# Attention's scores, values and gate filler as three streams through all heads, and a second buffer of squares in the projections of a hybrid block

## The chip, the core and the metric

The kernel runs on one core of one Trainium2 chip. The core has five engines, each with its own queue of instructions: TensorE (PE, matrix products and transposes, writing to PSUM), VectorE (DVE), ScalarE (ACT), GpSimd (POOL) and SyncE (SP, which issues the DMAs between memory and SBUF). The metric is the device time of one execution in microseconds (us); less is better. Times of runs are given as a median of several, and a profile is of one further execution.

## The reference

One layer of a streaming encoder over 1024 positions of width 1024, in float32:

```
hn = rms_norm(x);  u = hn @ w_in          # split for MLA, FoX, SSM and three gates
y_a = mla_branch(u_mla) @ w_br_mla        # 8 heads of 96, values of 64
y_b = fox_branch(u_fox) @ w_br_fox        # 8 heads of 64, decay added to the scores
y_c = ssm_branch(u_ssm) @ w_br_ssm        # conv, Mamba-2 scan, gated norm
g = sigmoid(u_gate + b_gate)
x = x + (g0 * y_a + g1 * y_b + g2 * y_c) @ w_out
x = x + conv_ffn(rms_norm(x))
```

Both attentions are a softmax over earlier positions (causal by chunks of 64 in MLA, strictly causal in FoX), `p = softmax(q k' + mask)`, `out = p v`. FoX normalises each head's q and k by the root of its mean square; z, the gate of the SSM branch, is a plain projection.

## The kernel before

All products keep float32's precision by splitting an operand into a high and a low part and adding three products. Lists of PE's instructions are in the order in which the program issues them (the stages run under a manual schedule for PE); the order on ACT, DVE, POOL and SP is made by the framework's scheduler from the program and its dependencies.

**Projections of FoX q, k and of z (lines 1016 to 1132).** Four column chunks of 512 (z first half, q, k, z second half) times eight token tiles: 32 units of 24 matmuls (`fx_part`, L798). Behind each unit of q or k, `qk_sum` squares the tile on ACT (L1053) into a buffer `fsq`, of which there is one, and sums it by heads on DVE (L1054). Behind each pair of tiles `qk_pair` makes 1/root of 16 columns on DVE (`rsqrt`, L157 to L168: two integer operations, a scaling and three Newton steps of three operations) and scales the tiles (L1063); `qk_out` transposes them on PE (L1070) into one of two `tp` banks, which ACT (L1074) and DVE (L1075) empty. `out_z` puts a tanh into the same buffer `fsq` (L1046). Beside the units run the split of the next chunk's weights (`load_part`; L139 on ACT, L140 on DVE), sums of weights for the last stage on POOL (`down_sums`, L939 to L942) and, in the third and fourth chunk, sums of the normalised input for the convolution (`token_sums`, L957 to L977, on POOL, ACT and DVE).

`small` (L246) is a tile of 128 x 8 x 24 numbers with the raw forget gates and time steps. It is last read at L836, before the units.

**Attention (L1403 to L1611).** 16 heads, the eight of MLA first. A head has four units `jp`, each of two rows of query tiles (128 queries). `score_row` computes the row's scores in one or two chunks (L1453) into one of two score banks `s`, with three products in MLA and two in FoX, where the mask is one more small product (L1463), held back until the next score row or values step. Then, through a list `later` of things to issue at nominal times: the row's maximum on DVE (L1464), the exponential with its sum on ACT (L1466) into one of six buffers `pm`, and 1/sum on DVE with the scaling on POOL (L1470, L1471). `values` transposes the two rows of a unit on PE (L1529) into two `tp` banks, groups of up to two key pairs at a time; ACT and DVE split them (L1534, L1535); products with the head's values `vv` follow two key pairs later (`PVLAG`; L1494 to L1502) into one bank `o` whose halves alternate; ACT and DVE empty it (L1507, L1512), and a DMA stores it to `att_d`.

The **filler** `all_fill` is the gate projection: 24 column blocks of two halves, each half eight steps of three matmuls (L1337), in pieces of two steps here. It has one bank, so that behind a half it yields up to four times without work until ACT has taken the bank (L1317). What attention doesn't use runs beside the SSD scan, and the rest alone behind it.

A generator yields the nominal cost of what it has just issued, in us. `merge` runs the streams of one unit to their end: always the one whose share of its own cost is least. A unit merges the scores of unit n, the values of unit n - 2, and fill for 0.50 of the two costs:

```
cost_s(jp, n=3) = sum(n * max(b - a, 256) / 2400 over the chunks of both rows) + 0.1
cost_v(jp)      = 0.88 * jp + 0.33 + 0.39
```

Over the four units of a head the columns sum to 4736, so that scores are 5.92 with three products and 3.95 with two; a FoX row yields 0.05 more than its products (`yield c + 0.05`, L1480). Values yield 0.11 for each transpose and 0.44 for each key pair's products. A fill step of three matmuls counts 0.65.

A head's q and k are loaded one head ahead, when the scores of unit 0 begin, and its `vv` when those of unit 3 begin (two buffers).

Of the kernel before, what the change touches and what calls it, by code (L numbers as in the profile page):

```python
# [11 lines left out]
F32 = mybir.dt.float32  # L12
# [9 lines left out]
P = 128  # L22
# [20 lines left out]
def block_kernel(ctx: ExitStack, tc: tile.TileContext, x, positions, norm_mix_g, w_in, b_gate,  # L43
# [951 lines left out]
    def conv_first():  # L995
# [17 lines left out]
        c_first["raw"], c_first["S"] = r, S_  # L1013
        yield

    with ExitStack() as px:
        xp = px.enter_context(TP("xp", 2))

        def load_part(w, n, j, c0):

# [21 lines left out]
            return lambda k: w[0][i][:, k, :] if k < 4 else w[k // 2 - 1][i][:, k % 2, :]  # L1042

        def out_z(p, t, zc):
            th = xp.tile([P, 512], F32, name=uid("th"), tag="fsq", bufs=1)
            A.activation(th, p, AF.Tanh, scale=0.5)  # L1046
            zt = xp.tile([P, 512], F32, name=uid("zt"), tag="fqn", bufs=4)
            V.scalar_tensor_tensor(out=zt, in0=th, scalar=1.0, in1=p, op0=ALU.add, op1=ALU.mult)
            SY.dma_start(z_d[t * P:(t + 1) * P, zc:zc + 512], zt)

        def qk_sum(p, ss):
            sq = xp.tile([P, 512], F32, name=uid("fsq"), tag="fsq", bufs=1)
            A.activation(sq, p, AF.Square)  # L1053
            V.reduce_sum(ss, sq.rearrange("p (h d) -> p h d", d=64), axis=AX)  # L1054

        def qk_pair(ps, ss):
            v = xp.tile([P, 16], F32, name=uid("fv8"), tag="fv8")
            V.tensor_scalar(v, ss, 1.0 / 64, EPS, op0=ALU.mult, op1=ALU.add)
            r = xp.tile([P, 16], F32, name=uid("fr8"), tag="fr8")
            rsqrt(xp, r, v, 16)  # L1060
            for i, p in enumerate(ps):
                qn = xp.tile([P, 8, 64], F32, name=uid("fqn"), tag="fqn", bufs=4)
                V.tensor_mul(qn, p.rearrange("p (h d) -> p h d", d=64),  # L1063
                             r[:, 8 * i:8 * i + 8].unsqueeze(2).to_broadcast([P, 8, 64]))
                yield qn
# [20 lines left out]
        for n, (which, c0) in enumerate(chunks):  # L1086
# [12 lines left out]
            for t in range(NT):  # L1099
# [13 lines left out]
                if which > 2:  # L1113
                    out_z(p, t, 512 * (which - 3))
                    if behind:
                        qk_out(*behind.pop(0))
                elif t % 2 == 0:
                    ss = xp.tile([P, 16], F32, name=uid("fss"), tag="fss")
                    qk_sum(p, ss[:, 0:8])
                    p_even = p  # L1120
                else:
                    qk_sum(p, ss[:, 8:16])
                    behind += [(qn, which, t - 1 + i) for i, qn in enumerate(qk_pair((p_even, p), ss))]
# [277 lines left out]
                s_[2] += c  # L1401


    class Head:
        pass

# [80 lines left out]
    def values(o, jp, pn, me):  # L1487
# [32 lines left out]
        for k0 in range(0, jp + 1, 2):  # L1520
# [3 lines left out]
            for kp in range(k0, min(k0 + 2, jp + 1)):  # L1524
                pt, pl = a_tp.get()
                off = 0
                for k in (2 * kp, 2 * kp + 1):
# [7 lines left out]
                pl[0] = later(cs + 0.6, lambda th=th, tl=tl, pt=pt, off=off: V.tensor_sub(  # L1535
                    tl[:, :off], pt[:, :off], f32(th[:, :off])))
                pend.append((pv, kp, th, tl, pl, jp, done if kp == jp else None))
            yield cs
            while len(pend) > PVLAG:
                if pend[0][1] == 0 and clk[0] - t_done[0] < 1.0:  # L1540
                    yield 0.0
                run_pv()
                if len(pend) <= PVLAG and k0 + 2 <= jp:
                    tp_next.append(me[0])
                yield 0.44

# [17 lines left out]
    def cost_v(jp):  # L1564
        return 0.88 * jp + 0.33 + 0.39

    FILL_ATT = 0.50
    FILL_SSD = [11.3] * 8 + [12.0, 24.5]
    with ExitStack() as pt__:
        atp = pt__.enter_context(TP("atp", 2))  # L1570
        psp = pt__.enter_context(TP("psa", 1, space=PSUM))
        a_pm = Ring(atp, [P, S], F32, "pm", 6)
        a_nmx, a_rs = (Ring(atp, [P, 4], F32, n, 4) for n in ("nmx", "rs"))
        a_th, a_tl = (Ring(atp, [P, 512], F32R, n, PVLAG + 2) for n in ("pth", "ptl"))
        a_o1 = Ring(atp, [64, 256], F32, "o1", 1)
# [4 lines left out]
        with tc.manual_schedule(engines={mybir.EngineType.PE}):  # L1580
            names = [(br, h) for br in range(2) for h in range(8)]
            merge([], 5.0)
            units = [(n, jp) for n in range(16) for jp in range(4)]
            heads = {0: load_head(atp, *names[0])}
            load_values(atp, heads[0])
            done = []
            for n in range(len(units) + 2):
                st, share = [], 0.0
                if n < len(units):
                    hn_, jp = units[n]  # L1590
                    if jp == 0 and hn_ + 1 < 16:
                        heads[hn_ + 1] = load_head(atp, *names[hn_ + 1])
                    if jp == 3 and hn_ + 1 < 16:
                        load_values(atp, heads[hn_ + 1])
                    pn = []
                    done.append((heads[hn_], jp, pn))
                    share += cost_s(jp)
                    st.append((scores(heads[hn_], jp, pn), cost_s(jp, len(heads[hn_].passes))))
                if n >= 2:
                    share += cost_v(done[n - 2][1])  # L1600
                    me = []
                    me.append(values(*done[n - 2], me))
                    tp_next[:] = me
                    st.append((me[0], cost_v(done[n - 2][1])))
                merge(st, FILL_ATT * share)
            flush()
            while pend:
                run_pv()
                clk[0] += 0.44
                run_until(clk[0])  # L1610
            run_until(clk[0] + 3.0)  # L1611
# [748 lines left out]
```

## Time and profile before

| | |
|---|---|
| runs, median (lowest to highest of 3) | 2035.72 us (2033.51 to 2036.61) |
| the profiled execution, its own time | 2032.95 us |
| its span, first to last instruction | 2031.2 us |
| granted TensorE clock, mean | 0.996 |
| busy: PE, DVE, ACT, POOL | 1974.9, 1403.3, 960.4, 720.4 us |
| projections of q, k and z, roughly | 197 to 401 us |
| attention | 516 to 918 us |

The page of the profile gives busy times by engine, the span in slices, the chain that ended last, and groups of instructions by line. In a group's row stand the line, engine, operation, the tile written and the tile read, the count, then busy us and the mean in ns of one, then the idle time of the engine before them and who ended it. A row of the waits reads: engine and line that waited, what released it, us in total, times, longest. A row of the timeline has start and duration in us and, in brackets, the engine's idle time before it. A row of the windows has the stretch, its length, then the busy time of each engine with its number of instructions, the granted clock, the share of the DMA engines and GB/s.

### The profile page before, as it was taken

The numbers are of one execution on the slowest core, as the hardware profiler recorded it, in microseconds if no ns is written. First come the engines' busy times: TensorE is split into PE (matmuls) and PEld (weight loads), VectorE is DVE, ScalarE is ACT, GpSimd is POOL, SyncE is SP. The second block draws the span as 40 slices with busy tenths as digits, with TensorE's granted clock in tenths as the row PEclk, the third lists the DMA queues.
The fourth block names the chain that finished last, engine by engine and source line by source line (L and its number), as shares of the span: only waits on it lengthen the run. The fifth ranks groups of instructions, "written<-read, shape, count | busy, mean of one in ns | idle before, by whom it ended". The sixth has DMA issues, their size and how long they took to land.

```text
span 2031.2 us, 28367 instructions
## 1 busy us (share of the span) xinstructions
PE 1974.9 (97%) x10113; PEld 1669.2 (82%) x10113; DVE 1403.3 (69%) x2141; ACT 960.4 (47%) x1674; POOL 720.4 (35%) x670
## 2 busy tenths in 40 slices
PE   9999997999899999999999999999999999999999
PEld 8999886788788887887888878888888888888887
DVE  7777579589566566665885466558997787675655
ACT  5554322345555556656775232224544445454432
POOL 5033335164222222222332163000565444522655
PEclk9999999999999999999999999999999999999999
DMA  5167873333644445526553687432422211249675
GB/s 176 61 195 219 266 249 95 108 102 104 180 128 128 127 127 140 143 79 215 179 178 125 215 294 257 145 125 84 135 83 84 93 58 46 84 134 330 205 258 193
DMA packets 278263, 312.15 MB, mean 154 GB/s; under 512 B 19197, under 2 KB 209289, under 8 KB 278122
## 3 DMA queue, kind: packets, MB, share of 16 engines
q1 hardware_dynamic: 278120, 310.35, 48.8%
q8 instruction: 79, 1.29, 0.3%
q14 instruction: 62, 0.51, 0.1%
q10 hardware_dynamic: 2, 0.00, 0.0%
HBM read 217.17 MB, written 93.13 MB: 153 GB/s over the span
## 4 chain that ended last, share of the span: by engine, by line
PE 81%; DVE 8%; ACT 3%; issue 3%; DMA 3%; POOL 1%; SPq 0%; ACTq 0%; DVEq 0%; POOLq 0%
PE mm L1337 12%; PE dn L2307 10%; PE ybr L1875 7%; PE fx L798 7%; PE ua L1966 5%; PE cb L1187 5%; PE uc L1966 5%; PE ud L1966 4%; PE wo L2011 4%; PE s L1453 3%; PE tp L1529 3%; PE ub L1966 2%; PE fxv L188 2%; PE py L1720 1%; ACT pm L1466 1%
## 5 line engine op out<-in xcount | busy, mean ns | idle before, releaser
L1471 POOL TENSOR_SCALAR pm<-pm,rs 128x128 f32<-128x128 f32 (+7 forms) x128 | 96.8, 757 | 298.7 <-DVE rs L1470 224.0
L2307 PE MATMUL dn<-dr,dr 128*128 128x512 f32 x592 | 182.3, 389 | 0.0
L1337 PE MATMUL mm<-hnh,wh 128*128 128x512 f32 x384 | 160.2, 417 | 0.9 <-DVE o L1512 0.9
L1337 PE MATMUL mm<-hnh,wl 128*128 128x512 f32 x384 | 151.2, 394 | 0.0
L1337 PE MATMUL mm<-hnl,wh 128*128 128x512 f32 x384 | 150.8, 393 | 0.0
L1535 DVE TENSOR_TENSOR ptl<-tp,pth 128x512 fp32r<-128x512 f32 (+1 forms) x160 | 98.6, 633 | 52.6 <-ACT pth L1534 50.9
L2307 PEld LDWEIGHTS dn<-dr,dr 128*128 128x128 f32 x592 | 111.1, 188 | 23.2
L1464 DVE TENSOR_REDUCE nmx<-s 128x1 f32<-128x128 f32 (+7 forms) x128 | 95.5, 752 | 32.9 <-PE s L1453 18.6
L2307 PE MATMUL dn<-dr 128*128 128x512 f32 x296 | 115.2, 389 | 0.0
L1466 ACT ACTIVATE pm<-s,nmx 128x128 f32<-128x128 f32 (+7 forms) x128 | 94.7, 742 | 43.2 <-DVE nmx L1464 34.4
L1534 ACT ACTIVATE pth<-tp 128x512 fp32r<-128x512 f32 (+1 forms) x160 | 85.1, 554 | 48.0 <-PE tp L1529 47.8
L135 DVE TENSOR_TENSOR dr<-dr,dr 128x1024 fp32r<-128x1024 f32 x52 | 72.1, 1395 | 51.8 <-ACT dr L134 41.0
L135 DVE TENSOR_TENSOR wl<-S,wh 128x1024 fp32r<-128x1024 f32 x53 | 80.7, 1523 | 32.7 <-ACT wh L134 32.7
L1875 PE MATMUL ybr<-ah,wl 128*128 128x512 f32 x256 | 99.7, 389 | 1.1 <-DVE wl L135 1.1
L1875 PE MATMUL ybr<-ah,wh 128*128 128x512 f32 x256 | 99.7, 389 | 0.4 <-ACT wh L134 0.4
L1875 PE MATMUL ybr<-al,wh 128*128 128x512 f32 x256 | 99.6, 389 | 0.0
L134 ACT ACTIVATE wh<-wr 128x1024 fp32r<-128x1024 f32 (+1 forms) x45 | 40.3, 896 | 103.3 <-PE ybr L1875 51.9
L134 ACT ACTIVATE dr<-dr 128x1024 fp32r<-128x1024 f32 x52 | 54.8, 1061 | 71.6 <-PE dn L2307 51.6
L134 ACT ACTIVATE wh<-S 128x1024 fp32r<-128x1024 f32 x53 | 56.1, 1059 | 63.8 <-PE uc L1966 45.7
L1337 PEld LDWEIGHTS mm<-hnh,wl 128*128 128x128 f32 x384 | 72.4, 189 | 16.6
L1529 PE MATMUL tp<-ident,pm 128*128 128x128 f32 x576 | 81.3, 273 | 2.0 <-DVE ptl L1535 1.6
L1337 PEld LDWEIGHTS mm<-hnh,wh 128*128 128x128 f32 x384 | 72.7, 189 | 12.4 <-DVE o L1512 1.1
(594 smaller groups left out, 6170.7 us busy)
## 6 DMA issues: line engine op xcount, KB each, us to landing
dr<-act_d SPq DMA_DIRECT2D x99, 256.0 KB
wr<-in_w_in_dram SPq DMA_DIRECT2D x36, 512.0 KB
g_d<-t SPq DMA_DIRECT2D x24, 512.0 KB
gl<-g_d SPq DMA_DIRECT2D x24, 512.0 KB
wr<-in_ffn_w_up_dram SPq DMA_DIRECT2D x23, 512.0 KB
ws<-in_ffn_w_down_dram SPq DMA_DIRECT2D x22, 512.0 KB
wsum_d<-ws SPq DMA_DIRECT2D x22, 512.0 KB
act_d<-fa SPq DMA_DIRECT2D x22, 512.0 KB
```

Of the source, the lines that this page charges most:

```text
L134: i = A.activation(h, src, AF.Copy) if he is A else he.tensor_copy(h, src)
L135: return i, le.tensor_sub(l, src, f32(h))
L798: T.matmul(p, a(k), b(k), start=k == 0 and i == 0, stop=k == NK - 1 and i == 2)
L1187: T.matmul(ps, a, b, start=first and i == 0, stop=i == 11, skip_group_check=not first)
L1337: T.matmul(ps, a[:, k, :], b[half][:, k, :], start=(k == 0 and i == 0), stop=(k == NK - 1 and i == 2))
L1466: pl[0] = later(t1, lambda: A.activation(p_[:, 0:n * P], row, AF.Exp, bias=nmx[:, 0:1], accum_out=rs[:, 0:1]))
L1471: G.tensor_scalar(p_[:, 0:n * P], p_[:, 0:n * P], rs[:, 1:2], 0.0, op0=ALU.mult, op1=ALU.add)
L1529: T.transpose(pt[:, off:off + P], pn[qi][0][:, k * P:k * P + P], ident)
L1535: pl[0] = later(cs + 0.6, lambda th=th, tl=tl, pt=pt, off=off: V.tensor_sub(tl[:, :off], pt[:, :off], f32(th[:, :off])))
L1875: T.matmul(pss[half], w_[:, k, :], a_[k][:, hs], start=k == 0 and i == 0, stop=k == nk - 1 and i == 2)
L1966: T.matmul(ps, a, b, start=first and n == 0, stop=n == 11, skip_group_check=not first)
L2307: T.matmul(ps[m], a[:, ts_], b[:, 512:], start=first_ and j == 0 and q == 0, stop=j == NFH - 1 and q == 2, skip_group_check=not first_)
```

## The change

Three edits. **In the projections** the buffer `fsq` gets a second copy. Room for it comes from the columns of the roots: `fv8`, `fr8`, `rs_i`, `rs_v`, `rs_t` and `fss`, 16 columns each in two copies, are now slices of the tile `small`, handed out in turn by a class `Columns`. **In attention** the units' merges give way to one call of `weave`: `all_scores` runs through the rows of all heads, `all_values` through the units' values, and the filler beside them. `weave` always advances the stream with the least account, where an account grows by what was yielded over the stream's cost of a head (`scores_`, `values_`, `FILL_HEAD` with 5.4 in MLA and 7.2 in FoX), and begins at 0 for scores, at 0.62 for values and at -0.6 for fill. A stream that yields 0 lets the least of the others go once. Values can't start a unit before both of its score rows are placed. While a FoX mask is held, values go first if they are due within 0.04 heads. It ends when only fill is left. **The buffers** `pm` grow from six to eight. In `values`, the stream is marked as next also where no products are due behind a group's transposes.

```diff
--- before.py
+++ after.py
@@ -1013,8 +1013,22 @@
         c_first["raw"], c_first["S"] = r, S_
         yield
 
+    class Columns:
+
+
+        def __init__(self, t):
+            self.flat, self.tags, self.turn = t.rearrange("p t c -> p (t c)"), {}, {}
+
+        def tile(self, shape, dt, name, tag):
+            i = self.tags.setdefault(tag, len(self.tags))
+            self.turn[tag] = j = 1 - self.turn.get(tag, 1)
+            c0 = 16 * (2 * i + j)
+            t = self.flat[:, c0:c0 + 16]
+            return t if dt is F32 else t.bitcast(dt)
+
     with ExitStack() as px:
         xp = px.enter_context(TP("xp", 2))
+        xs_ = Columns(small)
 
         def load_part(w, n, j, c0):
 
@@ -1042,22 +1056,22 @@
             return lambda k: w[0][i][:, k, :] if k < 4 else w[k // 2 - 1][i][:, k % 2, :]
 
         def out_z(p, t, zc):
-            th = xp.tile([P, 512], F32, name=uid("th"), tag="fsq", bufs=1)
+            th = xp.tile([P, 512], F32, name=uid("th"), tag="fsq")
             A.activation(th, p, AF.Tanh, scale=0.5)
             zt = xp.tile([P, 512], F32, name=uid("zt"), tag="fqn", bufs=4)
             V.scalar_tensor_tensor(out=zt, in0=th, scalar=1.0, in1=p, op0=ALU.add, op1=ALU.mult)
             SY.dma_start(z_d[t * P:(t + 1) * P, zc:zc + 512], zt)
 
         def qk_sum(p, ss):
-            sq = xp.tile([P, 512], F32, name=uid("fsq"), tag="fsq", bufs=1)
+            sq = xp.tile([P, 512], F32, name=uid("fsq"), tag="fsq")
             A.activation(sq, p, AF.Square)
             V.reduce_sum(ss, sq.rearrange("p (h d) -> p h d", d=64), axis=AX)
 
         def qk_pair(ps, ss):
-            v = xp.tile([P, 16], F32, name=uid("fv8"), tag="fv8")
+            v = xs_.tile([P, 16], F32, name=uid("fv8"), tag="fv8")
             V.tensor_scalar(v, ss, 1.0 / 64, EPS, op0=ALU.mult, op1=ALU.add)
-            r = xp.tile([P, 16], F32, name=uid("fr8"), tag="fr8")
-            rsqrt(xp, r, v, 16)
+            r = xs_.tile([P, 16], F32, name=uid("fr8"), tag="fr8")
+            rsqrt(xs_, r, v, 16)
             for i, p in enumerate(ps):
                 qn = xp.tile([P, 8, 64], F32, name=uid("fqn"), tag="fqn", bufs=4)
                 V.tensor_mul(qn, p.rearrange("p (h d) -> p h d", d=64),
@@ -1115,7 +1129,7 @@
                     if behind:
                         qk_out(*behind.pop(0))
                 elif t % 2 == 0:
-                    ss = xp.tile([P, 16], F32, name=uid("fss"), tag="fss")
+                    ss = xs_.tile([P, 16], F32, name=uid("fss"), tag="fss")
                     qk_sum(p, ss[:, 0:8])
                     p_even = p
                 else:
@@ -1401,6 +1415,29 @@
                 s_[2] += c
 
 
+    def weave(streams):
+
+        st = [[g, lead, per] for g, lead, per in streams]
+        while any(e[0] is not fill for e in st):
+            s_ = min(st, key=lambda e: e[1])
+            if held:
+                v = [e for e in st if e[0] in tp_next]
+                if v and v[0][1] <= s_[1] + 0.04:
+                    s_ = v[0]
+                else:
+                    flush()
+            c = advance(s_[0])
+            if c == 0.0:
+                rest = [e for e in st if e is not s_]
+                if rest:
+                    s_ = min(rest, key=lambda e: e[1])
+                    c = advance(s_[0])
+            if c is None:
+                st.remove(s_)
+            else:
+                s_[1] += c / s_[2]()
+
+
     class Head:
         pass
 
@@ -1535,12 +1572,14 @@
                 pl[0] = later(cs + 0.6, lambda th=th, tl=tl, pt=pt, off=off: V.tensor_sub(
                     tl[:, :off], pt[:, :off], f32(th[:, :off])))
                 pend.append((pv, kp, th, tl, pl, jp, done if kp == jp else None))
+            if len(pend) <= PVLAG:
+                tp_next.append(me[0])
             yield cs
             while len(pend) > PVLAG:
                 if pend[0][1] == 0 and clk[0] - t_done[0] < 1.0:
                     yield 0.0
                 run_pv()
-                if len(pend) <= PVLAG and k0 + 2 <= jp:
+                if len(pend) <= PVLAG:
                     tp_next.append(me[0])
                 yield 0.44
 
@@ -1564,12 +1603,13 @@
     def cost_v(jp):
         return 0.88 * jp + 0.33 + 0.39
 
-    FILL_ATT = 0.50
+    FILL_HEAD = (5.4, 7.2)
+    LAG = 0.62
     FILL_SSD = [11.3] * 8 + [12.0, 24.5]
     with ExitStack() as pt__:
         atp = pt__.enter_context(TP("atp", 2))
         psp = pt__.enter_context(TP("psa", 1, space=PSUM))
-        a_pm = Ring(atp, [P, S], F32, "pm", 6)
+        a_pm = Ring(atp, [P, S], F32, "pm", 8)
         a_nmx, a_rs = (Ring(atp, [P, 4], F32, n, 4) for n in ("nmx", "rs"))
         a_th, a_tl = (Ring(atp, [P, 512], F32R, n, PVLAG + 2) for n in ("pth", "ptl"))
         a_o1 = Ring(atp, [64, 256], F32, "o1", 1)
@@ -1580,29 +1620,37 @@
         with tc.manual_schedule(engines={mybir.EngineType.PE}):
             names = [(br, h) for br in range(2) for h in range(8)]
             merge([], 5.0)
-            units = [(n, jp) for n in range(16) for jp in range(4)]
             heads = {0: load_head(atp, *names[0])}
             load_values(atp, heads[0])
-            done = []
-            for n in range(len(units) + 2):
-                st, share = [], 0.0
-                if n < len(units):
-                    hn_, jp = units[n]
-                    if jp == 0 and hn_ + 1 < 16:
-                        heads[hn_ + 1] = load_head(atp, *names[hn_ + 1])
-                    if jp == 3 and hn_ + 1 < 16:
-                        load_values(atp, heads[hn_ + 1])
-                    pn = []
-                    done.append((heads[hn_], jp, pn))
-                    share += cost_s(jp)
-                    st.append((scores(heads[hn_], jp, pn), cost_s(jp, len(heads[hn_].passes))))
-                if n >= 2:
-                    share += cost_v(done[n - 2][1])
-                    me = []
-                    me.append(values(*done[n - 2], me))
-                    tp_next[:] = me
-                    st.append((me[0], cost_v(done[n - 2][1])))
-                merge(st, FILL_ATT * share)
+            todo = []
+            at = [0, 0]
+
+            def all_scores():
+                for n in range(16):
+                    at[0] = n // 8
+                    for jp in range(4):
+                        if jp == 0 and n + 1 < 16:
+                            heads[n + 1] = load_head(atp, *names[n + 1])
+                        if jp == 3 and n + 1 < 16:
+                            load_values(atp, heads[n + 1])
+                        pn = []
+                        todo.append((heads[n], jp, pn))
+                        yield from scores(heads[n], jp, pn)
+
+            me = []
+
+            def all_values():
+                for n in range(64):
+                    at[1] = n // 32
+                    while n >= len(todo) or len(todo[n][2]) < 2:
+                        yield 0.0
+                    yield from values(*todo[n], me)
+
+            me.append(all_values())
+            tp_next[:] = me
+            scores_ = lambda: sum(cost_s(jp, 3 - at[0]) - 0.1 for jp in range(4))
+            values_ = lambda: sum(cost_v(jp) for jp in range(4))
+            weave([(all_scores(), 0.0, scores_), (me[0], LAG, values_), (fill, -0.6, lambda: FILL_HEAD[at[1]])])
             flush()
             while pend:
                 run_pv()
```

## The prediction

> **What bounds the kernel now.** I read the page first: TensorE is the engine that is nearly always busy, so time can only come from stretches in which it stands still, or from the order of its own work.
>
> ```profile
> span 2031.2 us, 28367 instructions
> PE 1974.9 (97%) x10113; PEld 1669.2 (82%) x10113; DVE 1403.3 (69%) x2141; ACT 960.4 (47%) x1674; POOL 720.4 (35%) x670
> ```
>
> Then the busy time by stretch: 305 to 362 us is the middle of the FoX and z projections (two rows), 520 to 918 us is attention, with the MLA heads in the first of its two rows and the FoX heads in the second, to within a head. Columns: length, then busy time of PE, PEld, DVE, ACT, POOL, then the granted clock.
>
> ```profile
> 305.00:335.00 30.00, 24.64 (x111) 20.06 (x110) 28.93 (x39) 8.93 (x13) 18.87 (x10) 0.94 0.39 114
> 335.00:362.00 27.00, 17.37 (x76) 13.76 (x75) 26.52 (x47) 4.30 (x7) 9.76 (x3) 0.87 0.27 68
> 520.00:720.00 200.00, 188.16 (x1155) 163.11 (x1155) 119.70 (x244) 113.78 (x253) 47.89 (x65) 0.98 0.47 132
> 720.00:918.00 198.00, 189.52 (x1233) 160.17 (x1231) 124.66 (x251) 118.99 (x264) 48.94 (x64) 1.00 0.45 119
> ```
>
> PE stands idle for 15.0 us of the 57 in the projections, where **DVE** is full (55.5 of 57), and for 20.3 us of the 398 in attention, where ACT and DVE are each about 60% busy. The change edits these two stages alone; all others keep their instructions. The waits of PE in attention, and one of them in the timeline:
>
> ```profile
> PE s L1453 <- ACT pm L1466: 13.5, 18, 4.4
> PE o L1494 <- DVE o L1512: 2.4, 7, 0.4
> PE tp L1529 <- DVE ptl L1535: 1.6, 8, 0.3
> PE o L1494 <- ACT o L1507: 1.1, 4, 0.5
> ...
> 896.98 0.73 PE L1453 MATMUL s<-qk,qk 128*128 128x512 f32 x2 [0.59 <-ACT pm L1466]
> ```
>
> Without the single 4.4 us at the start, 9.1 us of scores waiting for the exponential of two rows before (two score banks), and 5.1 us of the values stream: 14.2 us are all that an even order could win there. To each wait come 0.16 us, because a matmul's shown end lies that much behind the point where the next can start (further down, two matmuls that start at 902.50 and are shown as 0.62 are followed by the mask 0.46 later); with 37 waits after the first, 6 us more. So at most some 20 us.
>
> **The attention, part by part.** I call "account" what a stream has done by its own count, in heads. The fill: before, 0.50 of the units' nominal cost, 16 heads at 0.5 x (5.92 + 0.4 + 8.16), 115.8, and 5.0 ahead, 120.8 nominal us. After, the fill's account runs from -0.6 to 16.8 heads, at 5.4 a head until values have reached head 8 (at 8.8) and 7.2 behind: 50.8 + 57.6 + 5.0 = 113.4. So some 7 us of fill leave attention. They don't vanish: all 24 gate blocks must be made, and what is left runs behind the SSD stage in one piece, as the last 60 matmuls of it do now. Net nothing, but it is cover that attention loses.
>
> ```profile
> 951.51 5.49 PE mm L1337 x24
> ...
> 1111.32 13.65 PE mm L1337 x60
> ```
>
> From the first row also the ratio of real to nominal time: 8 steps of 0.65 are 5.2, and take 5.49: 1.056.
>
> The wait of 4.4 us at the start stays: fill's lead of 0.6 heads looks like cover for it, but fill has one bank, and behind its first half yields four times without work, so that score rows 0 to 3 go first, as now, and row 2 waits for the same late exponential.
>
> Score waits: a head's rows are now spread by their cost over its 20.5 us, (5.92 + 8.16 + 5.4) x 1.056 in MLA and as much in FoX. The rows that wait now (row 6 for row 4) get a distance of 0.22 heads, 4.4 us, against the 2.4 that even row 5 below takes to the end of its exponential: gone. New is the turn of the head: row 1 of the next head needs row 7's exponential, and starts 0.16 heads, 3.3 us, behind row 7's last chunk, which needs 3.1 (0.69 + 1.22 + 1.11, below, and hops). I take 0.3 us a head, 5 in all. 5 - 9.1 - 17 x 0.16 is **-7**. The values' waits hang on two tp banks and on one bank of o for both halves, which stay: I take half, **-2.5**. DMAs: the same loads and stores; a head's vv now asks for the buffer of two heads before about 0.2 heads (4 us) before its last product frees it, so on SP's queue it can hold up the att_d stores (four o2 buffers) and the next wr load; none is due within those 4 us, so nothing; if one were, each head would pay up to 4 us, which the upper end doesn't hold. The eight pm buffers just reach: row 6 is written behind the transposes of the row eight before, which PE's order has directly ahead.
>
> **What the streams' accounts do.** This is the term that decides. PE's order is written by these accounts: the stream that is least far in heads goes next. But what a stream yields isn't what its divisor says. MLA scores yield 5.92 a head against 5.92. FoX scores yield 3.95 + 8 x 0.05 = 4.35 against 3.95: they lose 10% a head. Values yield 0.88jp + 0.77 a unit, 8.36 a head against 8.16: they lose 2.45%. So values, which start 0.62 heads behind, stand at (8 - 0.62)/1.0245 = 7.20 when scores reach head 8, 0.80 behind; and when scores end (account 16.81), values are at 15.80: **only 0.2 heads behind**. The distance melts through the FoX heads, while what has to fit into it does not. What that is, from the last FoX head of the trace: row 7 from its last chunk to its normalised row, and (rows behind the "...") row 5:
>
> ```profile
> 902.50 0.62 PE L1453 MATMUL s<-qk,qk 128*128 128x512 f32 x2
> 902.96 0.23 PE L1463 MATMUL s<-mfox,identb 128*128 128x128 bf16 x1
> 903.23 1.22 DVE L1464 TENSOR_REDUCE nmx<-s 128x1 f32<-128x1024 f32 x1 [0.22 <-PE s L1463]
> 904.68 1.11 ACT L1466 ACTIVATE pm<-s,nmx 128x1024 f32<-128x1024 f32 x1
> 905.91 0.16 DVE L1470 RECIPROCAL rs<-rs 128x1 f32<-128x1 f32 x1 [0.40 <-ACT pm L1466]
> 906.24 1.13 POOL L1471 TENSOR_SCALAR pm<-pm,rs 128x1024 f32<-128x1024 f32 x1 [2.05 <-DVE rs L1470]
> 907.99 1.19 PE L1529 MATMUL tp<-ident,pm 128*128 128x128 f32 x8
> ...
> 895.81 0.51 PE L1453 MATMUL s<-qk,qk 128*128 128x384 f32 x2
> 896.43 0.96 DVE L1464 TENSOR_REDUCE nmx<-s 128x1 f32<-128x768 f32 x1 [0.48 <-PE s L1463]
> 897.48 0.90 ACT L1466 ACTIVATE pm<-s,nmx 128x768 f32<-128x768 f32 x1 [0.55 <-DVE rs L1470]
> 898.76 0.91 POOL L1471 TENSOR_SCALAR pm<-pm,rs 128x768 f32<-128x768 f32 x1 [0.41 <-DVE rs L1470]
> ```
>
> Row 7: 0.69 to the mask's end, 1.22, then 2.69 from the exponential's start to POOL's end, and two hops of 0.05: 4.7 us. Row 5: 0.58 + 0.96 + 2.19 + 0.1 = 3.85. Before, a whole unit lies between (902.50 to 907.99 is 5.5), so the transposes never wait for POOL. After: the last chunk of row 7 of head n is placed at account 8 + 1.101(n - 8) + 0.98, the first transposes of its values at 0.62 + 1.0245(n + 0.592). The differences are 0.44 for head 8, then 0.37, 0.29, 0.21 (head 11), 0.135, 0.06, and below zero for 14 and 15, where values wait in the generator until the chunk is placed and follow at once. Into one head's account go values and fill of (8.16 + 7.2) x 1.056 = 16.2 us; with the chunk's own 0.5 the gap is 4.2 us in head 11, 2.7, 1.5, 0.5, 0.5. PE then waits 0.5 + 2.0 + 3.2 + 4.2 + 4.2 = 14.1 us. The same for row 5 and its transposes: differences 0.15, 0.08, 0 in heads 13 to 15, gaps 2.9, 1.65, 0.4, waits 0.95 + 2.2 + 3.45 = 6.6. In MLA the differences are 0.33 to 0.51 heads, 6 us and more: no wait. Together **+20.7**. PE is in order, so behind a waiting transpose stand fill and scores that could run, and behind those the next exponentials. Bounds: 0 if the distance doesn't melt; +33 if each chain meets queues as full as in the MLA part.
>
> Such waits may cost the clock too. The wait at the start, by stretch (length, PE busy, clock) and in the timeline:
>
> ```profile
> 527.00:533.00 6.00, 5.85 (x17) 0.53 0.78 216
> 533.00:540.00 7.00, 6.18 (x36) 1.00 0.00 0
> ...
> 527.15 2.61 PE L1453 MATMUL s<-w0h,w0l 104*128 104x384 f32 x6 [4.41 <-ACT pm L1466]
> 530.41 0.63 PE L1337 MATMUL mm<-hnh,wl 128*128 128x512 f32 x1
> ```
>
> After 4.41 us of idleness the next 6 us ran at a clock of 0.53, a loss of 2.8 us. The waits of 4.2 us in heads 14 and 15 are nearly that long; I count one such loss, **+2.8**, between 0 and four (11). The Trainium skill ("TensorE: Matmul & The Clock Gate", Part 1) puts the clock at half behind an idle window of about 3.4 us; this wait agrees, and by that rule three of mine are long enough and the term would be 8.4.
>
> **The projections.** A second buffer lets ACT square a tile while DVE still has to sum the one before. It waited for that:
>
> ```profile
> ACT fsq L1053 <- DVE fss L1054: 30.6, 4, 15.4
> PE fx L798 <- DVE w5l L140: 8.0, 1, 8.0
> PE tp L1070 <- DVE fsl L1075: 7.0, 2, 5.4
> ...
> 256.41 0.17 DVE L158 TENSOR_SCALAR fr<-rs_i 128x16 int32<-128x16 int32 x1
> 305.09 2.41 POOL L957 TENSOR_TENSOR Tf<-hnl 128x1024 f32<-128x1024 f32 x1
> 305.19 2.33 DVE L158 TENSOR_SCALAR fr<-rs_i 128x16 int32<-128x16 int32 x1
> ```
>
> But PE waits for DVE alone, 15.0 us, and DVE is full there: the same operation of 16 columns takes 0.17 us alone and 2.33 beside POOL's 2.4 us sums, and the twelve of a root stand in that. Squares made earlier take no work off DVE. What can change is the order: T3h comes earlier on ACT, so POOL's second sums start some 5 us earlier, and other DVE work meets them. I take **-3**; bounds -20 (all idle, and the clocks of 0.94 and 0.87) and +5. The root columns move into the dead tile: 6 names x 2 x 16 = 192 columns, exactly its 8 x 24. All are written and read on DVE, in its order, so no wait is added.
>
> **Sum**, against the profiled execution's own time (2032.95, the span and 1.75 around it): -7 - 2.5 + 20.7 + 2.8 - 3 = +11.0, **2044.0**. The median of the runs, 2035.72, lies 2.8 above the profiled one; I leave that in the range.
>
> **The rivals.** (a) *The distance is enough*: the transposes wait under 1 us in heads 11 to 15, because ACT and DVE, forced ahead, finish the chain within the fill and values between. Then only the gains count, up to -20 of waits, 5 back at the turn of the head, -3: 2033 - 18 is **2015**; with half the gains 2024. It decides from the point where the gap in head 13 reaches 4.7 us instead of 1.5. For it: scores and values each keep their own order, and 60% busy engines have room; against it: the accounts above, which are plain arithmetic. (b) *It cancels*: half of the melting and its clock loss (10.3 + 2.8) against the gains of the sum (12.5): **2034**. (c) *The second buffer is what counts*: 15 us of idle PE and the low clock go, DVE's order being better: **2018**; against it DVE's 55.5 of 57. (d) *It does nothing* in the projections and the streams only move the waits: **2033**, counted with (b).
>
> **How the numbers follow.** Slower by the melting distance 0.50; (a) 0.24 and (c) 0.08, both faster; (b) and (d) 0.18. A measurement of this kernel can tell about 0.2%, 4 us, from no change. The range: 2017 leaves out the best part of (a), 2060 takes in the queues' 12 us more and two more clock losses. By itself the likeliest case spans 2038 to 2060.
>
> **What would show it.** Right: a new line in which PE tp waits for POOL pm, absent before, with single waits of 2 to 4 us in the last four heads and none in MLA; waits of s for pm down to a few us; FoX heads that grow longer towards the end; the projections' idle still near 15 us, with ACT's 30.6 gone. Wrong: no such line, or equal FoX heads; or DVE well below full between 305 and 362 us.

## The result, and the profile after

After the change the kernel takes **2088.42 us** (2085.03 to 2089.59, 4 runs) against 2036.16 before (2033.51 to 2038.01): a ratio of 1.0255 [1.0237, 1.0273]. The forecast was 2044.0 with a range of 2017 to 2060. The sign and the leading mechanism came out as forecast; the size is five times as large, and the time lies 28 us above the range. The span of the profiled execution went from 2031.2 to 2086.3 us, +55.1. First the page's span, TensorE's row and the group of the values' transposes (its last field: PE's idle time ahead of them, and who ended most of it):

```profile
span 2086.3 us, 28385 instructions
PE 1995.2 (96%) x10113; PEld 1686.5 (81%) x10113; DVE 1407.0 (67%) x2141; ACT 965.0 (46%) x1674; POOL 725.1 (35%) x670
...
L1566 PE MATMUL tp<-ident,pm 128*128 128x128 f32 x576 | 87.5, 284 | 38.0 <-POOL pm L1508 33.1
```

The number of matmuls is the same, and PE is busy 20 us *longer*: some ran at a lower clock. Now the windows of the kernel after: the projections (two rows), the MLA heads, the FoX heads, the SSD stage with the filler that is left, and last the FoX heads cut in two.

```profile
305.00:335.00 30.00, 25.07 (x113) 20.43 (x112) 29.32 (x39) 9.54 (x13) 19.41 (x10) 0.94 0.38 115
335.00:362.00 27.00, 17.92 (x78) 14.24 (x77) 26.43 (x47) 4.14 (x7) 9.36 (x3) 0.88 0.27 68
520.00:716.00 196.00, 178.39 (x1097) 156.33 (x1097) 116.32 (x236) 110.96 (x246) 47.40 (x63) 0.97 0.45 123
716.00:960.00 244.00, 207.12 (x1240) 173.25 (x1238) 127.00 (x256) 123.08 (x270) 49.79 (x65) 0.93 0.39 102
960.00:1180.00 220.00, 213.07 (x1143) 180.94 (x1144) 148.66 (x190) 141.24 (x291) 64.94 (x79) 0.99 0.54 174
...
716.00:806.00 90.00, 87.75 (x575) 74.11 (x574) 58.21 (x121) 56.43 (x128) 23.78 (x31) 1.00 0.57 147
806.00:960.00 154.00, 119.37 (x666) 99.14 (x664) 68.79 (x136) 66.65 (x143) 26.00 (x34) 0.89 0.28 75
```

and the same cut of the kernel before, whose three stages are 196, 202 and 207 us long:

```profile
520.00:716.00 196.00, 184.16 (x1125) 159.46 (x1125) 117.25 (x236) 110.90 (x247) 45.78 (x62) 0.98 0.46 128
716.00:918.00 202.00, 193.52 (x1261) 163.82 (x1261) 127.10 (x259) 121.87 (x271) 51.05 (x66) 1.00 0.47 123
918.00:1125.00 207.00, 200.97 (x1096) 170.57 (x1095) 144.35 (x189) 138.53 (x287) 59.82 (x79) 1.00 0.56 180
```

The projections' rows stand almost as before, and MLA keeps its length. The FoX heads grow by 42 us, all of it in their last 154 us, where PE is idle for 35 us and the clock is 0.89; up to 806 us PE is as full as before. The SSD stage grows by 13 us. The waits of PE in the FoX heads (first four rows) and in the MLA heads (last three) of the kernel after:

```profile
PE tp L1566 <- POOL pm L1508: 33.1, 16, 3.9
PE o L1531 <- DVE o L1549: 1.3, 4, 0.5
PE tp L1566 <- DVE ptl L1572: 1.3, 2, 1.2
PE s L1490 <- ACT pm L1503: 0.3, 1, 0.3
...
PE s L1490 <- ACT pm L1503: 7.6, 5, 4.4
PE o L1531 <- DVE o L1549: 6.1, 5, 1.6
PE tp L1566 <- DVE ptl L1572: 3.6, 4, 1.6
```

The first row is the line that the prediction named. One of its waits, in the timeline (from the last chunk of a head's row 7 to the transposes of the unit that needs it):

```profile
808.54 0.64 PE L1490 MATMUL s<-qk,qk 128*128 128x512 f32 x2
809.55 1.21 DVE L1501 TENSOR_REDUCE nmx<-s 128x1 f32<-128x1024 f32 x1
810.26 0.28 PE L1566 MATMUL tp<-ident,pm 128*128 128x128 f32 x1
810.85 1.11 ACT L1503 ACTIVATE pm<-s,nmx 128x1024 f32<-128x1024 f32 x1 [0.74 <-DVE nmx L1501]
812.09 0.16 DVE L1507 RECIPROCAL rs<-rs 128x1 f32<-128x1 f32 x1 [0.87 <-ACT pm L1503]
812.42 1.12 POOL L1508 TENSOR_SCALAR pm<-pm,rs 128x1024 f32<-128x1024 f32 x1 [2.55 <-DVE rs L1507]
813.59 0.48 PE L1566 MATMUL tp<-ident,pm 128*128 128x128 f32 x1 [3.06 <-POOL pm L1508]
```

Hardly anything is queued in this chain: the maximum starts 0.3 us behind the mask's end, but then ACT stood idle until the maximum came, DVE until the exponential, POOL until the reciprocal. It is 5.05 us long, and PE had some 2 us of work to put into it.

To divide the stages I took the starts of successive matmuls from the trace. For each line and shape I call the distance "usual" than which a fifth are shorter. Excess over it of more than 0.6 us is a wait, smaller excess at half clock is clock, and the rest are short waits.

| us, before / after | length | usual distances | waits | half clock | rest |
|---|---|---|---|---|---|
| MLA | 194.0 / 194.4 | 168.8 / 161.7 | 8.1 / 19.1 | 2.6 / 6.4 | 14.5 / 7.1 |
| FoX | 202.4 / 244.3 | 178.9 / 175.4 | 7.4 / 38.4 | 0 / 15.2 | 17.1 / 16.1 |
| SSD, filler's end | 206.5 / 219.7 | 197.5 / 208.2 | 5.8 / 5.9 | 0 / 1.5 | 2.3 / 3.2 |

The first column grows by 55.5 us, which is the whole loss. The usual distances add up to the same (+0.1): 16 of the filler's steps, about 11 us (forecast: 7), have moved from attention to the stages behind it. Waits and half clock make +42 and +20, and shorter waits give 7 back.

### The profile page after: what moved, and what is told of

Same layout as the page of the kernel before. It is cut to its first block, busy times and chain, and to the rows that moved or that the text cites. A ratio compares the mean times of both kernels' runs of the same rounds, so it can differ in the third digit from the quotient of the medians.

```text
span 2086.3 us, 28385 instructions
## 1 busy us (share of the span) xinstructions
PE 1995.2 (96%) x10113; PEld 1686.5 (81%) x10113; DVE 1407.0 (67%) x2141; ACT 965.0 (46%) x1674; POOL 725.1 (35%) x670
## 4 chain that ended last, share of the span: by engine, by line
PE 78%; DVE 8%; issue 4%; ACT 4%; DMA 3%; POOL 2%; SPq 0%; ACTq 0%; DVEq 0%; POOLq 0%
PE dn L2355 10%; PE mm L1351 10%; PE ybr L1923 7%; PE fx L798 7%; PE ua L2014 5%; PE cb L1201 5%; PE uc L2014 5%; PE ud L2014 4%; PE wo L2059 4%; PE s L1490 4%; PE tp L1566 3%; PE ub L2014 2%; PE fxv L188 2%; PE o L1531 1%; ACT pm L1503 1%
## 5 line engine op out<-in xcount | busy, mean ns | idle before, releaser
L1508 POOL TENSOR_SCALAR pm<-pm,rs 128x512 f32<-128x512 f32 (+7 forms) x128 | 97.2, 761 | 343.8 <-DVE rs L1507 323.1
L1351 PE MATMUL mm<-hnl,wh 128*128 128x512 f32 x384 | 155.4, 405 | 0.0
L1566 PE MATMUL tp<-ident,pm 128*128 128x128 f32 x576 | 87.5, 284 | 38.0 <-POOL pm L1508 33.1
L1503 ACT ACTIVATE pm<-s,nmx 128x512 f32<-128x512 f32 (+7 forms) x128 | 94.7, 740 | 57.3 <-DVE nmx L1501 50.7
L1566 PEld LDWEIGHTS tp<-ident,pm 128*128 128x128 f32 x576 | 68.5, 145 | 47.4 <-POOL pm L1508 36.5
L134 ACT ACTIVATE dr<-dr 128x1024 fp32r<-128x1024 f32 x52 | 55.1, 1061 | 71.6 <-PE dn L2355 48.0
```

What stands on the lines that cost most here:

```text
L1351: T.matmul(ps, a[:, k, :], b[half][:, k, :], start=(k == 0 and i == 0), stop=(k == NK - 1 and i == 2))
L1503: pl[0] = later(t1, lambda: A.activation(p_[:, 0:n * P], row, AF.Exp, bias=nmx[:, 0:1], accum_out=rs[:, 0:1]))
L1508: G.tensor_scalar(p_[:, 0:n * P], p_[:, 0:n * P], rs[:, 1:2], 0.0, op0=ALU.mult, op1=ALU.add)
L1566: T.transpose(pt[:, off:off + P], pn[qi][0][:, k * P:k * P + P], ident)
```

## The experiments

The theory: FoX's waits come from the streams' distance melting, since values and scores yield more per head than their divisors say, and the chain of row 7 (maximum, exponential, reciprocal, scaling) no longer fits. Rivals: it is the thinner filler (5.4 a head in MLA), the merge over all heads as such, or the projections. All ratios are against runs of the kernel before on the same chip (medians of 2033.7 to 2034.2).

**Accounts made even, and a larger distance.** (Run `e1_even`.) The divisors get what the streams really yield.

```diff
-    LAG = 0.62
+    LAG = 0.80
...
-            scores_ = lambda: sum(cost_s(jp, 3 - at[0]) - 0.1 for jp in range(4))
-            values_ = lambda: sum(cost_v(jp) for jp in range(4))
+            scores_ = lambda: sum(cost_s(jp, 3 - at[0]) - 0.1 for jp in range(4)) + 0.4 * at[0]
+            values_ = lambda: sum(cost_v(jp) + 0.05 for jp in range(4))
```

> The changed kernel with accounts that count what the streams yield (FoX scores 4.35 a head, values 8.36) and with values 0.80 heads behind, so that the distance between scores and values stays near 0.69 heads through all 16 heads. Theory (the melting distance): the 33 us in which PE's transposes wait for POOL's normalised rows go to under 3 us, with them the nine stretches of half clock in the FoX heads; FoX heads take 23 us each to the end; time 2042 to 2050. Rival (less filler as cover, or the order of the streams as such): the waits stay and the time is above 2075.

Measured 2048.94, ratio 1.0075 [1.006, 1.009]. No transpose waits for POOL any more; its FoX heads are 203 us at clock 1.00. What is left in attention, from the waits and the windows of FoX and SSD:

```profile
PE o L1531 <- DVE o L1549: 9.4, 15, 2.4
PE s L1490 <- ACT pm L1503: 8.5, 9, 4.4
PE tp L1566 <- DVE ptl L1572: 6.6, 9, 1.9
```

```profile
710.00:913.00 203.00, 191.23 (x1244) 162.27 (x1242) 125.37 (x257) 121.92 (x270) 48.74 (x65) 1.00 0.46 122
913.00:1138.00 225.00, 214.40 (x1142) 181.91 (x1143) 146.97 (x190) 140.75 (x290) 63.15 (x79) 0.98 0.52 170
```

So the two lines of accounts and the distance take back 1.8 of the 2.55 per cent. What stays shows in the waits for the one bank `o` (9.4 us against 3.5 before) and in a longer SSD stage (225 against 207), which also runs 16 steps of filler, about 11 us, that attention took before.

**Accounts made even, distance as in the change (0.62).** (Run `e2_even_062`.) Only the two divisors of above.

> The same accounts with values 0.62 heads behind, as in the changed kernel; the first two key pairs of products yield nothing, so that the distance is 0.51 heads from the first head to the last. Theory: it doesn't melt, but is short throughout: 3.3 to 3.8 us of work between row 7 and its transposes against 4.7 needed, so waits of about 1 us in nearly every head, 12 to 18 us in all, few of them long enough for the clock; time 2052 to 2066, between e1 and the changed kernel. Rival: like the changed kernel, 2080 to 2090.

Measured 2046.72, 1.0064 [1.0048, 1.0081]. That is below the expected range, and the waits are 3.0 us where I expected 12 to 18:

```profile
PE o L1531 <- DVE o L1549: 10.4, 12, 1.2
PE tp L1566 <- POOL pm L1508: 3.0, 7, 0.8
```

Even at 0.62 hardly anything is left. PE has 3.6 to 4.2 us of work, counted from the start of the chunk, in *every* FoX head, and with the short waits in between it takes 4.4 to 5.8 us to reach the unit's first transposes, against chains of 4.8 to 5.9. It is the melting that counts, far more than the distance at the start.

**The filler back.** (Run `e3_fill_back`.) The change with 7.24 a head throughout, so that attention uses as much of it as before.

```diff
-    FILL_HEAD = (5.4, 7.2)
+    FILL_HEAD = (7.24, 7.24)
```

> The changed kernel with the filler's share in attention as before (7.24 a head in both branches in place of 5.4 and 7.2). Rival (attention lost its cover): the time comes back to 2050 or less. Theory (the melting distance): in the FoX heads nothing changes, waits of transposes for POOL stay at 28 to 36 us; the MLA heads have 15 us more filler in which part of their waits for the bank of o go, and as much less runs behind the SSD scan; time 2078 to 2090.

Measured 2085.19, 1.0257 [1.024, 1.0274], the ratio of the change itself. The wait stands:

```profile
PE tp L1566 <- POOL pm L1508: 31.2, 18, 3.9
```

The rival "thinner filler" falls for the FoX waits: in heads 12 to 15 of this run, too, PE has no work left between a head's last chunk and the transposes of its last unit.

**The projections alone.** (Run `e4_projections`.) The kernel before with `Columns` and the second buffer, attention untouched; of the edit, the line for the squares:

```diff
-            sq = xp.tile([P, 512], F32, name=uid("fsq"), tag="fsq", bufs=1)
+            sq = xp.tile([P, 512], F32, name=uid("fsq"), tag="fsq")
```

> The kernel before with the second buffer of squares and the root columns in the dead tile, attention as before. Theory: DVE is full there, so PE's idle time stays near 15 us; time 2030 to 2037. Rival (the second buffer counts): 2018 to 2024.

Measured 2036.16, 1.0008 [0.9999, 1.0017]: nothing. The waits of the change in 300 to 365 us say why:

```profile
ACT fsq L1067 <- PE fx L798: 27.1, 6, 5.1
ACT fsq L1067 <- DVE small L1068: 5.8, 1, 5.8
PE fx L798 <- DVE w5l L140: 7.9, 1, 7.9
PE tp L1084 <- DVE fsl L1089: 6.1, 2, 4.9
```

ACT now waits mostly for PE; its wait for DVE's sum, which is written to a slice of `small` now, fell from 30.6 to 5.8 us. PE waits for DVE as before. Rival (c) falls.

**Melting faster.** (Run `e5_melt_more`.) The change with the values' divisor alone made right: values no longer lag by their 2.45% a head, scores still lose 10%.

```diff
-            values_ = lambda: sum(cost_v(jp) for jp in range(4))
+            values_ = lambda: sum(cost_v(jp) + 0.05 for jp in range(4))
```

> The changed kernel with the values' account corrected (8.36 a head) and the FoX scores' account not. Values then stay 0.51 heads behind in MLA instead of falling to 0.69, and all the melting of 0.10 a head comes off that. Theory: MLA as in e2, transposes wait for POOL from head 8 or 9 on, 4 us a head at unit 3, then 3.5 at unit 2 and from head 11 on at unit 1: 60 to 78 us of waits in all, with some 25 to 35 us of half clock; time 2115 to 2160. Rival (the waits come from something else than the distance): within 10 us of the changed kernel.

Measured 2136.61 (two runs), 1.0505 [1.0484, 1.0526].

```profile
PE tp L1566 <- POOL pm L1508: 64.7, 45, 3.9
...
711.00:1010.00 299.00, 232.56 (x1233) 194.84 (x1231) 128.62 (x255) 125.66 (x267) 48.81 (x65) 0.84 0.31 83
```

Twice the waits, at a clock of 0.84, by an edit that corrects one of two errors: they had partly made up for each other.

**The distance that I had reckoned with.** (Run `e8_lag_073`.) Values start 0.11 heads nearer than 0.62 says (why, stands in the section on the reasons); with 0.11 more the distance is the one of the prediction's working.

```diff
-    LAG = 0.62
+    LAG = 0.73
```

> The changed kernel with values 0.73 instead of 0.62 heads behind, which puts back the 0.11 heads by which the first two key pairs of products, that yield nothing, bring values forward. This is the distance with which the waits were forecast. Theory: transposes wait for POOL 17 to 25 us, from head 11 on, with fewer stretches of half clock; time 2060 to 2075. Rival (the forecast's chain of 4.7 us was too short, not its distance too long): waits of 30 us and more, time 2080 and above.

Measured 2062.6, 1.0141 [1.0126, 1.0156].

```profile
PE tp L1566 <- POOL pm L1508: 17.3, 8, 3.9
...
706.00:935.00 229.00, 204.26 (x1271) 171.04 (x1270) 128.89 (x261) 123.04 (x272) 49.74 (x65) 0.96 0.42 110
```

17.3 us against a term of 20.7 (at row 7's unit 12.4 against 14.1, at row 5's 5.0 against 6.6): the price of the chain was nearly right, the distance was not. But this kernel is still 28 us slower than the one before, where the forecast had 11, so the distance is not the whole error: half clock costs 8.3 us in FoX against 2.8 forecast, and the values' waits (`o`, `ptl`) are 10.3 us, twice those before instead of half.

**The values' wait for bank `o`.** (Run `e6_o_wait`.) Even accounts at 0.62; a unit's first product may now step aside three times instead of once.

```diff
-                if pend[0][1] == 0 and clk[0] - t_done[0] < 1.0:
-                    yield 0.0
+                for _ in range(3):
+                    if pend[0][1] == 0 and clk[0] - t_done[0] < 1.4:
+                        yield 0.0
```

> e2_even_062, and before the first products of a unit up to three steps of other streams (instead of one) while the bank of o was finished less than 1.4 nominal us ago. Theory: the 10 to 11 us in which products wait for the bank of o fall below 4, the rest stays; time 2036 to 2043. Rival (the wait only moves): within 3 us of e2.

Measured 2043.83, 1.0046 [1.0029, 1.0062], 3 us below the kernel without it, with intervals that overlap. DVE's share of the wait fell from 10.4 to 7.0 us, not below 4 as expected. Most of the wait stayed, and what it gave up is worth 3 us at most, so it was not the main rest.

**Even accounts with more distance and more filler** (run `e7_o_wait_far`): the edit of before, `LAG` 0.72 and `FILL_HEAD` (6.3, 7.2).

> e6_o_wait with values 0.72 instead of 0.62 heads behind and 6.3 instead of 5.4 of filler in an MLA head. Theory: the few us of transposes that wait for POOL go, MLA has more cover; time 2032 to 2041, level with the kernel before. Rival: as e6.

Measured **2029.3**, 0.9973 [0.9964, 0.9983]: better than expected, far faster than the changed kernel, and 0.27% faster than the one before. Its windows:

```profile
520.00:711.00 191.00, 180.61 (x1127) 159.24 (x1127) 116.74 (x237) 111.66 (x247) 47.58 (x63) 0.99 0.48 133
711.00:910.00 199.00, 189.94 (x1254) 162.04 (x1253) 126.78 (x257) 121.88 (x270) 50.64 (x65) 1.00 0.47 122
910.00:1118.00 208.00, 202.68 (x1099) 172.52 (x1098) 143.28 (x189) 140.01 (x288) 57.77 (x79) 0.99 0.56 180
```

Three more runs take its parts apart. The same with one step aside (run `e9_far_one_yield`):

> e7_o_wait_far with one step instead of three ahead of a unit's first products, as in the changed kernel. If the bank of o counts: 3 us slower than e7, as e6 was 3 us faster than e2: 2030 to 2034. If distance and filler make e7's gain: as e7, 2027 to 2032.

2030.57, 0.9987 [0.9978, 0.9997], with 9.3 us of waits for `o` on DVE against 6.4: at best a us or two, and the intervals touch. The same with `LAG` 0.62 (run `e10_o_wait_062`):

> e7_o_wait_far with values 0.62 heads behind, as in e6; filler 6.3 and 7.2. If the distance makes the gain over e6: transposes wait for POOL 3 us again, time 2038 to 2044. If the filler in MLA does: 2029 to 2034.

2031.77, 0.999 [0.998, 0.9999]. So of the 14.5 us between the last kernel at 5.4 (run `e6_o_wait`) and the best one (`e7_o_wait_far`), 12.1 come with filler at 6.3; the 2.5 that come with the distance are not clear, as the intervals overlap. The same with filler (7.24, 7.24) (run `e11_fill_724`):

> e7_o_wait_far with the kernel before's filler (7.24 a head in both). If cover in MLA counts on: 2021 to 2027. If 6.3 was enough: within 3 us of e7. With the melting gone and the same filler in attention as before, this is the three streams against the units' merges alone.

2028.91, 0.9973 [0.9961, 0.9984]: no more to win. Attention takes 200 steps of filler in this kernel, 190 in `e7_o_wait_far` and 192 in the kernel before, so at like filler the ratio is about what streams through all heads are worth once they are even: 0.27%, some 5 us of the at most 20 that the prediction allowed. The other parts of the change (the second buffer, eight `pm`, the mark in `values`) and the three steps aside are in this figure too; of these, only the second buffer and the steps aside were tried alone.

The filler thus does matter when the streams are even. At 5.4 the MLA heads have less to put between the values' products. Compare the stages of the kernel at 5.4 with three steps aside and of the best one (MLA, FoX and SSD: 188.9, 199.3, 226.6 and 189.9, 198.6, 207.9 us). In attention the usual distances grow by 9 us and the waits fall by 11, and its length stays the same: attention takes in 14 more steps of filler, about 10 us, for nothing. Of the SSD stage's 19 us, 10 are that filler; the others are stalls and half clock of that stage, which get fewer as well. One of them in the waits of PE there, first in the kernel at 5.4, then in the best:

```profile
PE stp L1701 <- issue: 6.1, 2, 3.3
```

```profile
PE stp L1701 <- issue: 3.1, 1, 3.1
```

Why a transpose of the scan stands for 3 us with no releaser, twice or once, was not settled.

## Why the prediction was right in kind and wrong in size

| term | forecast | measured | from |
|---|---|---|---|
| score waits | -7 | -5.6 | 13.5 before; 7.6 and 0.3 after |
| values' waits (`o`, `ptl`) | -2.5 | +7.4 | 5.1 before; 12.5 after (6.1, 3.6, 1.3, 1.3, and 0.2 for ACT) |
| melting distance | +20.7 | +33.1 | the new line |
| clock | +2.8 | +20.5 | 3.8 MLA, 15.2 FoX, 1.5 SSD |
| projections | -3 | -0.7 | up to the end of the convolution |
| filler moved | 0 | +0.1 | usual distances |
| sum | +11.0 | +54.8 | span: +55.1 |

(The forecast's -7 held the short gaps at each wait too; measured, the "rest" of the stages fell by 7.5, and waits of over 0.6 us that no row above holds take about as much back.)

Of the 43.8 us between the two sums, 17.7 lie in the clock, 12.4 in the melting distance and 9.9 in the values' waits.

**Melting: right, and mis-sized in one step.** A line in which transposes wait for POOL appeared, with single waits of up to 3.9 us, none in MLA, and FoX heads that grew from about 23 to 32 to 35 us. What failed is the step "the first transposes of its values at 0.62 + ...". Products follow their transposes two key pairs late, so the first two key pairs yield nothing: the values' account stands 0.88/8.16 = 0.108 heads lower at each transpose than I wrote, and that much nearer to scores through all heads. The rule by which values go first within 0.04 heads of a held mask, which I had read and not counted, could bring them up to 0.04 nearer still; no run tries it alone, and the measured work doesn't ask for it. Work of PE in the chain of row 7, by head, in us of usual distances and with the chunk's own 0.5:

| head | 8 | 9 | 10 | 11 | 12 | 13 | 14 | 15 |
|---|---|---|---|---|---|---|---|---|
| as forecast | 7.6 | 6.5 | 5.2 | 4.2 | 2.7 | 1.5 | 0.5 | 0.5 |
| with 0.108 heads less | 5.9 | 4.7 | 3.4 | 2.2 | 1.0 | 0.5 | 0.5 | 0.5 |
| measured, kernel after | 6.7 | 4.5 | 3.4 | 1.3 | 0.5 | 0.5 | 0.5 | 0.5 |
| measured, run at 0.73 | 8.0 | 7.6 | 4.5 | 4.1 | 2.9 | 1.0 | 0.5 | 0.5 |

(The forecast's 4.2 in head 11 is a slip: its difference of 0.21 gives 3.9, and the term 0.3 more.) With the 0.108 heads taken off, the prediction's own arithmetic gives some 31 us of waits, 20 for row 7 and 11 for row 5. Of the 33.1 measured, 18.5 stand at row 7's unit, 11.6 at row 5's, and 3.0 at row 3's in heads 14 and 15, which the prediction didn't count. The run at 0.73 is the other half of the proof: with the 0.11 heads given back, the work is close to the forecast's row and the waits are 17.3 us.

**Clock: the step "I count one such loss" failed, and it is the largest miss.** There were nine stretches at half clock in FoX, two in MLA beside the one at the start, and one in SSD, where the bound was four (11 us). I went by a wait of 4.4 us; less is enough (last section). In the run at 0.73, at the forecast's own distance, four of the eight waits for POOL, those of 3.1 us and more, were followed by half clock, so one loss was too few even for the waits that I forecast.

**Values' waits: wrong in sign.** I took half of 5.1 away, with no trace behind the half. In MLA they grew from 2.3 to 9.7 us. The thinner filler has part in this: in the run whose only edit puts the filler back, the same rows of MLA add up to 6.3 us, and MLA's waits by the starts to 13.5 against 19.1. That it lets a unit's products come closer behind those before in the one bank `o` is my reading and was not tried by itself. The stage doesn't get longer, since 7 us of filler left it and short waits fell.

**Projections: right that DVE is the limit**; -0.7 against -3. PE's idle time there is 14.0 of 57 us against 15.0. "T3h comes earlier" brought nothing that can be measured (1.0008).

**The rivals.** (a) needed a gap of 4.7 us in head 13; it was 0.5, the chunk itself. (b) fails with it. (c) falls with the projections alone. Of (d), the projections' half held. The slower kernel was given 0.50 and came; the range ended at 2060 because it held the queues' 12 us and two more clock losses, but no error of the distance itself, the term on which all hung.

## What to carry to other kernels

Where an order is written by accounts, add up what each stream really yields, from its first step (what is deferred yields nothing yet), and follow the difference of the accounts to the end: 0.11 heads were 16 us of waits and some 24 us of time here. Accounts made even by themselves cut the loss from 2.55% to 0.64%, and with more filler in MLA besides, the streams gain 0.1 to 0.27%. Ask of a distance between streams how much *work* lies in it at its smallest, against the longest chain that must fit. And price a repeated wait on TensorE with its clock: 0.35 to 0.5 us for each us waited, in the FoX heads of three kernels here (15.2 on 38.4, 38.6 on 74.6, and 8.3 on 24.0 at 0.73).

## What the runs showed of the hardware

**A period of 3.413 us that is only half busy halves the clock of the next.** The times at which the clock fell in the attention of the kernel after (642.00, 665.89, 812.66, 846.80, 867.28, ... 952.61) all lie on one grid of 3.413 us. Windows cut along it (length, PE busy, clock, and last the DMA engines' share and GB/s):

```profile
638.58:642.00 3.42, 1.78 (x14) 1.00 0.51 159
642.00:645.41 3.41, 3.41 (x13) 0.50 0.99 254
...
809.25:812.66 3.41, 1.19 (x8) 1.00 0.61 129
812.66:816.07 3.41, 2.48 (x10) 0.50 0.89 201
816.07:819.49 3.42, 3.42 (x14) 0.50 0.37 101
819.49:822.90 3.41, 3.41 (x25) 1.00 0.55 219
833.15:836.56 3.41, 1.81 (x15) 1.00 0.65 192
836.56:839.97 3.41, 3.41 (x23) 1.00 0.00 0
843.39:846.80 3.41, 0.62 (x6) 1.00 0.70 143
846.80:850.21 3.41, 3.41 (x13) 0.50 1.00 181
```

Behind a period with 1.78, 1.19 or 0.62 us of work comes one at 0.50; behind 1.81 none. The half clock lasts until a period has been nearly full: with 2.48 us at half clock behind 812.66 it went on, with 3.42 it ended. (In the six kernels of the next sentence it always went on up to 0.77 of a period and always ended above 0.88.) Over the attention of six kernels (before, after, and the runs with even accounts, filler back, faster melting and 0.73), no period at full clock with PE busy for 0.51 or less of it failed to halve the next, none above 0.56 did, and in between both occur. The Trainium skill ("TensorE: Matmul & The Clock Gate", Part 1) speaks of an idle window of about 3.4 us, running freely: the period and the grid agree, but the window need not be idle; here 1.64 us of standstill within one was enough. By the rule as I read it, three of my waits were long enough; nine stretches at half clock came in FoX, 34.1 us in all, and cost 15.2 us on top of the waits.

**A chain with hardly a queue in it.** Each link of the softmax chain of a row is short (1.21, 1.11, 0.16 and 1.12 us), and DVE and ACT are more than half idle in the last 154 us of FoX, but the chain takes 4.7 to 5.1 us from the chunk's start. In head 15 of the kernel before, PE had 4.3 us of work behind the chunk and did not wait; in heads 12 to 15 of the kernel after it had none and stood for 3.7 to 3.9 us a head.
